# Value pass of a hybrid decoder block: the split weights of a pair of blocks, one block behind the other in place of side by side

## The chip, the cores and the metric

The kernel runs on one core of one Trainium2 chip. The core has a matrix engine (TensorE, PE in the profile; its weight loads have a row of their own, PEld), VectorE (DVE), ScalarE (ACT), GpSimd (POOL) and a queue engine (SyncE, SP) that issues transfers; 16 DMA engines move data between memory and the core's on-chip memory of 128 partitions. The metric is the device time of one launch in microseconds. Before the change it was 1544.01 us, the median of three runs (1541.96 to 1545.22).

## What is computed

One layer of a decoder block for 256 tokens of width 2048: sparse attention beside a convolution, a projection, a layer norm, then an expert channel mixer and a second layer norm. The change lies in the mixer. Each token picks, for each of 8 heads, 16 of 16384 experts; an expert has a row of `u_tab` and a row of `v_tab`.

```python
def peer_ffn(y, wq, sub_keys, u_tab, v_tab):
    ...
        top, pos = lax.top_k(cand, PK_TOPK)
        eidx = jnp.take_along_axis(cidx, pos, axis=-1)
        g = jax.nn.softmax(top.astype(jnp.float32), axis=-1)
        u = u_tab[eidx]
        v = v_tab[eidx]
        h = jax.nn.gelu(jnp.einsum('btd,bthkd->bthk', yb, u))
        return jnp.einsum('bthk,bthkd->btd', g * h, v).astype(y.dtype)
```

The second einsum is the value pass: for each token, the sum of its 128 chosen rows of `v_tab`, each with its weight `g * h`.

## The kernel before

The kernel goes through the mixer in three stages. The u pass reads all of `u_tab` in 128 blocks of 128 experts. The middle stage finds the weights and spreads them into a dense matrix. The value pass multiplies that matrix with all of `v_tab`.

The dense matrix is `W = wp.tile([P, T, P], F32)`: partition, 256 tokens `t`, 128 blocks `j`. On one partition the 128 blocks of a token lie side by side, so two tokens of the same block are 128 elements, 512 bytes, apart. Block `j` of the value pass takes the weights `W[:, t, j]` of all 256 tokens and the 128 rows of `v_tab` that belong to it. The first 768 columns of `v_tab` are not multiplied densely: they are gathered row by row and summed. The other 1280 (`VC`) go through TensorE, cut into pieces of 512, 512 and 256 columns (`blocks`).

TensorE works in a one-pass format (`F32R`), so each operand is split into a high part and the remainder. `mm3` (L330 to L332) multiplies high by high, high by low and low by high. In the profile's names, L330 is `wh` with `vh`, L331 `wh` with `vl`, L332 `wl` with `vh`. The weights are the stationary operand: each matmul first loads 128 columns, one for each of 128 tokens, and then streams 512 or 256 columns of V. A block has 2 token halves x 3 pieces x 3 products = 18 matmuls; the result tiles are `f` (512 wide) and `fboth` (256 wide).

One turn `j` of the loop, in the order in which the program gives work to the engines, which each engine keeps:

- `v_load(j + 2)`: SP issues the transfer of the rows of block `j + 2` into `vr` (L1768, 640 KB, three buffers); POOL issues two gathers into `gv` (L1776, one for each token half, 384 KB each, eight buffers).
- `v_split(j + 1)`: on even blocks `v_rows` comes first and makes the weights of two blocks at once, high part `wh` on ScalarE (L1805), remainder `wl` on VectorE (L1806). Then `v_cols` makes `vh` on ScalarE (L1816) and the remainder `vl`, 1024 columns on VectorE and 256 on POOL (both L1821).
- `v_gather(j)`: VectorE adds the two gathered tiles into `pg` (L1781).
- `v_use(j)`: the 18 matmuls.

`vh` and `vl` have one buffer in each of two pools, used in turn by `j % 2`; `wh` and `wl` likewise by pair, `p % 2`. So `vh` of block `j + 1` waits until TensorE has finished with block `j - 1`, and a `vr` buffer is free when `vh` and both parts of `vl` have been made from it. Nine blocks (`AHEAD`) have one gather fewer in the loop; it was done ahead.

Of the kernel before, what the change touches and what calls it, by code (L numbers as in the profile page):

```python
# [10 lines left out]
F32R = mybir.dt.float32r  # L11
# [9 lines left out]
P = 128  # L21
T = 256
# [96 lines left out]
def tile_hybrid_block(  # L119
# [6 lines left out]
    x = x[0]  # L126
# [202 lines left out]
    def mm3(acc, ah, al, bh, bl, start, stop):  # L329
        nc.tensor.matmul(acc, lhsT=ah, rhs=bh, start=start, stop=False)  # L330
        nc.tensor.matmul(acc, lhsT=ah, rhs=bl, start=False, stop=False)  # L331
        nc.tensor.matmul(acc, lhsT=al, rhs=bh, start=False, stop=stop)  # L332
# [591 lines left out]
    if True:  # L924
# [14 lines left out]
        for c in range(8):  # L939
# [6 lines left out]
            src = raws[i][:, r * 512:r * 512 + 512]  # L946
# [408 lines left out]
    if True:  # L1355
# [96 lines left out]
        for h in range(1, PH):  # L1452
            for half in range(2):
                p = 2 * h + half
# [67 lines left out]
    W = wp.tile([P, T, P], F32, name="W")  # L1522
# [274 lines left out]
    halves_ = {}  # L1797

    def v_rows(p, tt):
        if p not in halves_:  # L1800
            halves_[p] = [vps[p % 2].tile([P, T, 2], F32R, name=f"w{x}{p}", tag=f"w{x}") for x in "hl"]
        s = slice(0, T) if tt is None else slice(tt * P, tt * P + P)
        wh, wl = (t[:, s] for t in halves_[p])
        src = W[:, s, 2 * p:2 * p + 2]
        nc.scalar.activation(wh, src, AF.Copy)  # L1805
        nc.vector.tensor_tensor(wl, src, wh.bitcast(F32), op=OP.subtract)  # L1806

# [15 lines left out]
    def v_split(j):  # L1823
        if j % 2 == 0:
            v_rows(j // 2, None)
        v_cols(j, slice(0, VC))
# [77 lines left out]
    if True:  # L1904
# [77 lines left out]
        for m in range(NQ - QP, NQ, 2):  # L1982
# [16 lines left out]
            if m == NQ - 12:  # L1999
                v_raw(2)  # L2000
                v_rows(0, 0)
# [7 lines left out]
            if m == NQ - QP + 2:  # L2009
# [5 lines left out]
                vps = [psv.enter_context(tc.tile_pool(name="vp0", bufs=1, reuse_waits="tile", side="right"))]  # L2015
# [6 lines left out]
    if stop == "u":  # L2022
        dump("hv", hv)
        if "H" in dbg:
# [6 lines left out]
    acc = [[psv_.tile([P, 512], F32, name=f"f{tt}{b}", tag=f"f{tt}{b}") for b in range(nb - 1)]  # L2031
           for tt in range(2)]
# [9 lines left out]
    def v_part(j, tt, b, stop=False):  # L2042
        (wh, wl), vhl = halves_[j // 2], parts[j]
        (a, e), s = blocks[b], slice(tt * P, tt * P + P)
        mm3(acc[tt][b], wh[:, s, j % 2], wl[:, s, j % 2], vhl[0][:, a:e], vhl[1][:, a:e],
            j == 0 and not (tt and b == nb - 1), stop)

    def v_use(j, tts=range(2)):
        for b in range(nb):
            for tt in tts:  # L2050
                v_part(j, tt, b)
# [10 lines left out]
    z2 = []  # L2062
    if True:
        v_rows(0, 1)
        for j in range(P):
            if j == 1:
# [8 lines left out]
            elif len(z2) < 2:  # L2075
                tt = len(z2)
# [35 lines left out]
        for j in (P - 2, P - 1):  # L2112
            for b in range(nb):
                v_part(j, 0, b, j == P - 1 and b < nb - 1)
        residual(nb - 1)
        for j in (P - 2, P - 1):
            v_part(j, 1, nb - 1, j == P - 1)
# [144 lines left out]
```

## Time and profile before

| What | Value |
|---|---|
| median of three runs | 1544.01 us |
| the profiled execution | 1547.76 us |
| its span (first to last instruction) | 1545.9 us |
| PE, PEld, DVE, ACT, POOL busy, of the span | 97, 89, 88, 55, 67% |
| granted TensorE clock, mean | 0.996 |
| DMA, mean over the span | 308 GB/s |
| first matmul of the value pass | 1052.9 us |
| last matmul of the value pass on these weights | 1534 us |

The stages, in us of the span, with the time that each engine was busy in them:

| Stage | us | PE | DVE | ACT | POOL | DMA share | GB/s |
|---|---|---|---|---|---|---|---|
| up to the u pass | 0 to 480 | 471.28 | 378.85 | 257.00 | 198.43 | 0.56 | 200 |
| u pass | 480 to 900 | 415.57 | 387.55 | 275.90 | 316.03 | 0.99 | 384 |
| middle | 900 to 1052 | 148.97 | 134.67 | 115.87 | 115.99 | 0.72 | 232 |
| value pass | 1052 to 1534 | 470.41 | 443.66 | 202.91 | 400.50 | 0.98 | 376 |
| last norm and output | 1534 to 1546 | 0.86 | 8.35 | 1.47 | 6.69 | 0.48 | 175 |

Matmuls overlap in the records: the next one starts before the last one's recorded end. A stage in which PE is "busy" nearly all the time may therefore still have room; the distance from one start to the next tells more. A wait is put down to what came last. The DMA share is the mean busy share of the 16 DMA engines.

### The profile page before, as it was taken

Reading aid. Unit: us, or ns where it says so; the run is one execution under the profiler, and the core shown is the slowest. Engines: PE = TensorE matmul, PEld = TensorE weight load, DVE = VectorE, ACT = ScalarE, POOL = GpSimd, SP = SyncE. Lnnn points to the kernel's source line nnn. Section 1 sums busy time; section 2 is a strip of 40 time slices with the busy share of each in tenths; the row PEclk is TensorE's granted clock in tenths of the full one; section 3 lists DMA queues with packets and bytes.
Section 4 is the critical chain, followed back from the end, with each engine's and each line's share of the span. In section 5 each row is a group of like instructions: output and inputs, shape, how many; then the busy total and the mean of one; then the engine's idle time right before and its main releaser. Section 6 shows DMA issues by size and latency. Waiting matters only on the chain.

```text
span 1545.9 us, 29511 instructions
## 1 busy us (share of the span) xinstructions
PE 1507.1 (97%) x10932; PEld 1379.0 (89%) x10932; DVE 1353.1 (88%) x2381; ACT 853.1 (55%) x1207; POOL 1037.7 (67%) x897
## 2 busy tenths in 40 slices
PE   9999999999999999999999999999999999999996
PEld 9998999987999999999999888887878888888885
DVE  5999777857599998999998789988999999989898
ACT  5355776645434666666666657885444444444443
POOL 1886000053774777777877678767888888888883
PEclk9999999999999999999999999999999999999999
DMA  9664545255685999999999987757999999999997
GB/s 350 226 243 137 174 138 186 89 194 187 217 303 171 406 403 403 404 401 395 398 407 389 363 285 250 225 194 257 395 370 389 394 380 385 386 384 407 379 389 256
DMA packets 101492, 475.77 MB, mean 308 GB/s; under 512 B 17728, under 2 KB 20516, under 8 KB 92772
## 3 DMA queue, kind: packets, MB, share of 16 engines
q1 hardware_dynamic: 59300, 252.81, 44.1%
q0 software_dynamic: 41040, 218.60, 37.4%
q10 hardware_dynamic: 1008, 2.49, 0.4%
q8 instruction: 85, 1.39, 0.4%
q14 instruction: 59, 0.48, 0.1%
HBM read 468.99 MB, written 4.85 MB: 307 GB/s over the span
## 4 chain that ended last, share of the span: by engine, by line
PE 32%; DMA 12%; issue 9%; POOL 6%; DVE 6%; ACT 3%; DVEq 0%; SPq 0%; POOLq 0%; ACTq 0%
PE hp L1541 8%; PE hp L1537 8%; PE hp L1538 8%; DMA vr<-in_v_dense_dram 7%; POOL gv L1776 4%; PE bank L1703 4%; DVE pg L1781 3%; DMA gv<-in_v_rows_dram,e 3%; PE bank L1751 2%; POOL vl L1821 2%; DMA ur<-in_u_dense_dram 1%; DVE vl L1821 1%; ACT vh L1816 1%; PE bank L1733 1%; ACT slot L1739 1%
## 5 line engine op out<-in xcount | busy, mean ns | idle before, releaser
L1776 POOL DMA_INDIRECT gv<-in_v_rows_dram,e x256 | 292.2, 1141 | 67.5 <-issue 32.8
L1816 ACT ACTIVATE vh<-vr 128x1280 fp32r<-128x1280 f32 (+1 forms) x129 | 162.1, 1258 | 271.8 <-DMA vr<-in_v_dense_dram 199.7
L291 POOL TENSOR_TENSOR lo<-raw,hi 128x1024 fp32r<-128x1024 f32 (+1 forms) x76 | 171.8, 2273 | 166.0 <-ACT hi L273 165.4
L1537 PE MATMUL hp<-yh,uh 128*128 128x256 f32 x1152 | 280.6, 283 | 1.1 <-ACT uh L1240 1.1
L1538 PE MATMUL hp<-yl,uh 128*128 128x256 f32 x1152 | 280.1, 282 | 0.0
L1173 POOL DMA_INDIRECT gu<-in_u_rows_dram,e x196 | 192.8, 983 | 98.8 <-DVE gu L1183 62.3
L1781 DVE SCALAR_TENSOR_TENSOR pg<-gv,hv,pg 128x768 f32<-128x768 f32 x247 | 251.7, 1019 | 4.3
L1240 ACT ACTIVATE uh<-ur 128x1152 fp32r<-128x1152 f32 x128 | 149.6, 1168 | 130.6 <-PE hp L1538 45.6
L331 PE MATMUL f<-vl,wh 128*128 128x512 f32 x512 | 209.6, 409 | 10.8 <-DVE vl L1821 10.1
L1537 PEld LDWEIGHTS hp<-yh,uh 128*128 128x128 f32 x1152 | 217.8, 189 | 1.5 <-ACT uh L1240 1.5
L1538 PEld LDWEIGHTS hp<-yl,uh 128*128 128x128 f32 x1152 | 217.8, 189 | 0.0
L273 ACT ACTIVATE hi<-raw 128x1024 fp32r<-128x1024 f32 (+1 forms) x134 | 138.1, 1036 | 127.5 <-PE pwq L331 27.4
L1183 DVE SCALAR_TENSOR_TENSOR gu<-gu,yp 128x896 f32<-128x896 f32 x196 | 206.3, 1077 | 0.1
L330 PE MATMUL f<-vh,wh 128*128 128x512 f32 x512 | 204.4, 399 | 0.8 <-ACT vh L1816 0.8
L332 PE MATMUL f<-vh,wl 128*128 128x512 f32 x512 | 203.4, 397 | 0.0
L1821 DVE TENSOR_TENSOR vl<-vr,vh 128x1024 fp32r<-128x1024 f32 (+1 forms) x129 | 160.7, 1247 | 30.8 <-ACT vh L1816 30.0
L1541 PE MATMUL hp<-yh,ul 128*128 128x256 f32 x1152 | 157.8, 282 | 0.8 <-DVE ul L1245 0.8
L1245 DVE TENSOR_TENSOR ul<-ut,uh 128x768 fp32r<-128x768 f32 x126 | 119.6, 949 | 31.1 <-ACT ut L1244 22.9
L1541 PEld LDWEIGHTS hp<-yh,ul 128*128 128x128 f32 x1152 | 145.6, 188 | 1.2 <-DVE ul L1245 1.2
L1246 POOL TENSOR_TENSOR ul<-ur,uh 128x384 fp32r<-128x384 f32 x128 | 131.3, 1026 | 17.7 <-ACT uh L1240 15.1
L331 PEld LDWEIGHTS f<-vl,wh 128*128 128x128 f32 x512 | 100.1, 195 | 42.7 <-DVE vl L1821 27.3
L1821 POOL TENSOR_TENSOR vl<-vr,vh 128x256 fp32r<-128x256 f32 (+1 forms) x129 | 123.1, 954 | 12.8 <-ACT vh L1816 10.3
(390 smaller groups left out, 3857.9 us busy)
## 6 DMA issues: line engine op xcount, KB each, us to landing
vr<-in_v_dense_dram SPq DMA_DIRECT2D x128, 640.0 KB
ur<-in_u_dense_dram SPq DMA_DIRECT2D x128, 576.0 KB
raw<-in_w_pieces_dram SPq DMA_DIRECT2D x62, 1024.0 KB
gv<-in_v_rows_dram,e POOLq DMA_INDIRECT x256, 7.0
gu<-in_u_rows_dram,e POOLq DMA_INDIRECT x196, 6.8
raw<-in_w_pieces_dram SPq DMA_DIRECT2D x5, 512.0 KB
raw<-in_w_pieces_dram SPq DMA_DIRECT2D x4, 608.0 KB
w1k<-in_cmp_w_dram SPq DMA_DIRECT2D x1, 2048.0 KB
```

The source lines that it names most:

```text
L330: nc.tensor.matmul(acc, lhsT=ah, rhs=bh, start=start, stop=False)
L331: nc.tensor.matmul(acc, lhsT=ah, rhs=bl, start=False, stop=False)
L332: nc.tensor.matmul(acc, lhsT=al, rhs=bh, start=False, stop=stop)
L1173: nc.gpsimd.indirect_dma_start(out=gt, out_offset=None, in_=u_rows, in_offset=bass.IndirectOffsetOnAxis(ap=fl(e4, tt)[:, c:c + 1], axis=0))
L1183: nc.vector.scalar_tensor_tensor(gt, gt, 1.0, yr, op0=OP.mult, op1=OP.mult, accum_out=hv[:, tt, c:c + 1])
L1537: nc.tensor.matmul(acc, lhsT=uh[:, s], rhs=chunk(yh, k), start=k == 0, stop=False)
L1538: nc.tensor.matmul(acc, lhsT=uh[:, s], rhs=chunk(yl, k), start=False, stop=False)
L1541: nc.tensor.matmul(acc, lhsT=ul[:, s], rhs=chunk(yh, k), start=False, stop=k == UK - 1)
L1776: nc.gpsimd.indirect_dma_start(out=gvs[j, tt], out_offset=None, in_=v_rows_, in_offset=bass.IndirectOffsetOnAxis(ap=fl(e4, tt)[:, j:j + 1] ...
L1781: engine.scalar_tensor_tensor(pg[:, tt], gvs.pop((j, tt)), wv[:, tt, j:j + 1], pg[:, tt], op0=OP.mult, op1=OP.add)
L1816: nc.scalar.activation(vh, src[:, s], AF.Copy)
L1821: e.tensor_tensor(vl, src[:, c], vh.bitcast(F32), op=OP.subtract)
```

## The change

`wh` and `wl` of a pair of blocks were `[P, T, 2]`: for each token the weights of the two blocks side by side. They become `[P, 2, T]`: all 256 tokens of the first block, then all 256 of the second.

```diff
@@ def v_rows(p, tt):
-            halves_[p] = [vps[p % 2].tile([P, T, 2], F32R, name=f"w{x}{p}", tag=f"w{x}") for x in "hl"]
+            halves_[p] = [vps[p % 2].tile([P, 2, T], F32R, name=f"w{x}{p}", tag=f"w{x}") for x in "hl"]
         s = slice(0, T) if tt is None else slice(tt * P, tt * P + P)
-        wh, wl = (t[:, s] for t in halves_[p])
-        src = W[:, s, 2 * p:2 * p + 2]
+        wh, wl = (t[:, :, s] for t in halves_[p])
+        src = W[:, s, 2 * p:2 * p + 2].rearrange("p t j -> p j t")
         nc.scalar.activation(wh, src, AF.Copy)
         nc.vector.tensor_tensor(wl, src, wh.bitcast(F32), op=OP.subtract)
@@ def v_part(j, tt, b, stop=False):
-        mm3(acc[tt][b], wh[:, s, j % 2], wl[:, s, j % 2], vhl[0][:, a:e], vhl[1][:, a:e],
+        mm3(acc[tt][b], wh[:, j % 2, s], wl[:, j % 2, s], vhl[0][:, a:e], vhl[1][:, a:e],
             j == 0 and not (tt and b == nb - 1), stop)
```

So L1805 and L1806 read the same 512 elements of `W` in another order: before, for each token two neighbours; now, for one block all tokens and then for the other, each element 512 bytes behind the last. They write `wh` and `wl` from front to back in both versions. A weight load of TensorE read 128 elements 8 bytes apart; now it reads 128 neighbours. The tiles keep their size and buffers, and every engine has the same instructions in the same order. The first pair's weights are made in two steps of 128 tokens each (`v_rows(0, 0)`, `v_rows(0, 1)`); there the two blocks' parts are written 256 elements apart.

## The prediction

> **What bounds the kernel now.** The whole change lies in the value pass, so I read that stage by itself: its busy times in one window, the chain that ended last inside it (shares by line), and who waited for whom (us in total, times, longest).
>
> ```profile
> core 0: us, PE busy (x) PEld busy (x) DVE busy (x) ACT busy (x) POOL busy (x), PEclk, DMA share, GB/s
> 1060.00:1520.00 460.00, 449.05 (x2214) 377.39 (x2214) 426.17 (x430) 192.12 (x185) 394.33 (x364) 1.00 0.99 384
> ```
>
> ```profile
> by line: issue 27.4%; DMA vr<-in_v_dense_dram 24.4%; POOL gv L1776 12.4%; DVE pg L1781 8.9%; DMA gv<-in_v_rows_dram,e 8.6%; POOL vl L1821 6.9%; DVE vl L1821 3.4%; ACT vh L1816 2.7%; PE f L331 1.0%; PE f L332 0.9%; DMA z<-y_dram 0.9%; PE f L
> ```
>
> ```profile
> ACT vh L1816 <- DMA vr<-in_v_dense_dram: 199.7, 92, 3.8
> ACT vh L1816 <- PE fboth L332: 34.8, 16, 4.0
> PEld f L331 <- DVE vl L1821: 27.3, 58, 1.8
> PE f L331 <- DVE vl L1821: 10.1, 22, 1.5
> ```
>
> The first row is the steady part of the pass: DMA share 0.99, VectorE busy 426 of 460 us (93%), ScalarE only 192. PE shows 449, but matmuls overlap in the records, so its starts are counted below instead. The chain ("by line") hardly touches PE, some 1% for each of its lines; it runs through POOL's gather issues and the transfers of vr. The waits say the same: ScalarE waits 199.7 us for rows of V, 34.8 us for PE to release a buffer, and PE waits 27.3 + 10.1 us for VectorE's vl. One turn of the timeline (start in us, us taken, engine, line) shows how these hang together:
>
> ```profile
> 1302.14 0.66 ACT L1805 ACTIVATE wh<-W 128x512 fp32r<-128x512 f32 x1
> 1304.33 0.75 POOL L1821 TENSOR_TENSOR vl<-vr,vh 128x256 fp32r<-128x256 f32 x1
> 1305.11 0.33 SPq L1768 DMA_DIRECT2D vr<-in_v_dense_dram  x1
> 1305.24 0.96 POOL L1776 DMA_INDIRECT gv<-in_v_rows_dram,e  x1 [0.16 <-issue]
> 1305.40 0.68 DVE L1806 TENSOR_TENSOR wl<-W,wh 128x512 fp32r<-128x512 f32 x1
> 1306.23 1.22 DVE L1821 TENSOR_TENSOR vl<-vr,vh 128x1024 fp32r<-128x1024 f32 x1 [0.16 <-ACT vh L1816]
> 1306.50 1.77 POOL L1776 DMA_INDIRECT gv<-in_v_rows_dram,e  x1 [0.30 <-issue]
> 1308.29 0.76 POOL L1821 TENSOR_TENSOR vl<-vr,vh 128x256 fp32r<-128x256 f32 x1
> 1311.94 1.28 ACT L1816 ACTIVATE vh<-vr 128x1280 fp32r<-128x1280 f32 x1 [1.67 <-DMA vr<-in_v_dense_dram]
> ```
>
> The next vr is issued at 1305.11, just behind the end of POOL's vl (1304.33 + 0.75); the block it brings is converted at 1311.94, 6.83 us later. POOL's second gather took 1.77 us, not 0.96: it ran into VectorE's vl and ended 0.8 us behind it (1308.27 against 1307.45), and POOL's own vl came after. So **whatever delays VectorE's vl delays POOL, and through POOL the next transfer of V**.
>
> **What the change does, part by part.** No instruction is added, dropped or reordered on any engine. Three accesses change: ScalarE and VectorE write wh and wl contiguously, as before, but read W with one element every 512 bytes instead of two neighbours every 512 bytes; and TensorE loads its 128 weight columns 4 bytes apart instead of 8.
>
> **Read of W by VectorE.** Nothing in the trace is exactly this, so its neighbours, as groups (xcount, busy us, mean ns of one) and by tile (ns min/median/max):
>
> ```profile
> L1806 DVE TENSOR_TENSOR wl<-W,wh 128x512 fp32r<-128x512 f32 x63 | 43.8, 695 | 0.9 <-ACT wh L1805 0.9
> L1821 DVE TENSOR_TENSOR vl<-vr,vh 128x512 fp32r<-128x512 f32 x2 | 1.3, 672 | 0.0
> L482 DVE TENSOR_REDUCE csum<-conv 128x256 f32<-128x2048 f32 x1 | 3.9, 3851 | 0.5 <-ACT conv L469 0.5
> L763 DVE TENSOR_REDUCE st<-sc 128x4 f32<-128x1024 f32 x8 | 9.8, 1220 | 0.3
> L763 DVE TENSOR_REDUCE st<-sc 128x4 f32<-128x512 f32 x8 | 5.5, 686 | 0.3
> L570 DVE TENSOR_TENSOR blkk<-bk,small x8: 349/356/2534, 118.1 to 127.4; 128x120 f32<-128x120 f32 x8
> L710 DVE TENSOR_TENSOR csb<-csb,csm x4: 282/282/284, 198.0 to 284.5; 128x120 f32<-128x120 f32 x4
> ```
>
> Read in pairs, wl costs 695 ns, against 672 for the same subtraction on contiguous data: pairs are almost free. Single elements are not. L482 reads single elements 1 KB apart. The two L763 rows, contiguous, give (1220 - 686)/512 = 1.04 ns an element and 152 ns fixed, so its 2048 elements would take 2.29 us; it took 3.85, or 0.76 ns more for each. L570, a subtraction's sister with single reads 64 bytes apart, has a median of 356 ns where L710, of the same size, has 282: 0.62 ns more for each. On wl's 512 elements that is 0.39 or 0.32 us. I take **+0.35 us per wl**, between the two. The ends: 0, if a single read costs no more than a pair, and +0.53, if each element takes twice its 1.04 ns; it can hardly become faster, since wl stands 23 ns above the contiguous row.
>
> [...]
>
> **Read of W by ScalarE.** A wh starts at 1302.14 and ends at 1302.80; its wl starts at 1305.40. If it grew by 0.66 us, doubled, it would still end 1.9 us ahead. ScalarE is idle for 268 of the 460 us, over 2 us a block of some 3.7, so vh behind it is covered too: cost 0, and at most the doubling where a wh follows late.
>
> **What VectorE's 0.35 us does.** A pair of blocks on VectorE is one wl, two vl and four sums:
>
> ```profile
> 1254.24 0.68 DVE L1806 TENSOR_TENSOR wl<-W,wh 128x512 fp32r<-128x512 f32 x1
> 1254.84 1.22 DVE L1821 TENSOR_TENSOR vl<-vr,vh 128x1024 fp32r<-128x1024 f32 x1
> ...
> 1261.08 0.69 DVE L1806 TENSOR_TENSOR wl<-W,wh 128x512 fp32r<-128x512 f32 x1
> L1806 DVE TENSOR_TENSOR wl<-W,wh x63: 682/684/1142, 1057.8 to 1522.3; 128x512 fp32r<-128x512 f32 x63
> L1821 DVE TENSOR_TENSOR vl<-vr,vh 128x1024 fp32r<-128x1024 f32 x126 | 159.1, 1263 | 30.8 <-ACT vh L1816 30.0
> ```
>
> Without a gap a pair takes 1261.08 - 1254.24 = 6.84 us: VectorE's floor. The 63 wl stand (1522.3 - 1057.8)/62 = 7.49 us apart on average. The floor rises to 7.19, so VectorE alone is not the average bound, with 96% of the period taken instead of 91%. The cover is the idle time before vl, 30.8 us, or 0.5 us a pair. It isn't spread evenly: of the 62 periods between those wl starts, 27 are shorter than 7.19, and they fall short of it by 7.4 us in sum. These pairs are the ones that catch up behind a late transfer. If they are stretched to the new floor and nothing is made good later, the pass grows by 7.4 us; if the transfers (share 0.99) set the mean and a later issue only meets a shorter queue, by nothing; if every delay passes through, by 63 x 0.35 = 22 us. Since vr has three buffers and its next issue follows POOL's vl at once, I expect little to be made good: **+7 us**.
>
> **Weight loads of TensorE.**
>
> ```profile
> 324.74 0.40 PE L330 MATMUL mixb<-hi,ch 128*128 128x512 f32 x1
> 329.98 0.39 PE L332 MATMUL mixb<-hi,cl 128*128 128x512 f32 x1
> 1199.82 0.40 PE L331 MATMUL f<-vl,wh 128*128 128x512 f32 x1
> 1202.40 0.28 PE L330 MATMUL fboth<-vh,wh 128*128 128x256 f32 x1
> 1203.13 0.40 PE L330 MATMUL f<-vh,wh 128*128 128x512 f32 x1
> L330 PEld LDWEIGHTS mixb<-hi,ch x64: 186/188/192, 324.6 to 368.9; 128*128 128x128 f32 x64
> L330 PEld LDWEIGHTS f<-vh,wh x512: 192/195/329, 1052.9 to 1533.8; 128*128 128x128 f32 x171
> 700.66 0.28 PE L1537 MATMUL hp<-yh,uh 128*128 128x256 f32 x1
> 702.80 1.23 PE L1541 MATMUL hp<-yh,ul 128*128 128x256 f32 x9
> ```
>
> In the value pass a 512-wide matmul takes (1202.40 - 1199.82)/11 steps = 235 ns and a 256-wide one (1203.13 - 1202.40)/6 = 122. With contiguous weights the output projection's 512-wide ones take (329.98 - 324.74)/23 = 228, and the 256-wide ones of the u pass (702.80 - 700.66)/18 = 119; a weight load takes 188 ns there and 195 here. If the 8-byte step is the reason, a block's 12 wide and 6 narrow matmuls lose 12 x 7 + 6 x 3 = 0.10 us, 13 us over 128 blocks, and PE's floor for a pair falls from 2 x (12 x 0.235 + 6 x 0.122) = 7.10 us to 6.90. But PE has 3% of the chain, some 14 us, of which 7/235 is 0.4 us. Ends: 0, if something else makes 235 of 228, and -13, if PE set every block. I take **-0.5 us**.
>
> [...] The rows' 195 against 188 ns differ with the step, so I keep the row.
>
> At the start of the pass two 128x256 pieces of wh and wl are made on the way to the first matmul: 0.2 us at most, inside the rounding.
>
> **Sum.** +7 - 0.5 = +6.5 us. The profiled execution took 1547.8 us, so its like would take 1554.3; it lies 3.8 us above the median of the three runs, 1544.0. On that median the forecast is **1550 us**.
>
> **The rivals.**
>
> *The read costs nothing* (0.18). If single reads run at the pair's speed, or the layout reaches the engine in another order than written, VectorE is as before and PE gains off the path: 1543.5 us. For it: 695 against 672 ns shows VectorE swallowing 256 jumps. Against: L482 and L570.
>
> *PE's release sets the pace* (0.12), the other side. ScalarE waited 16 times for PE to free vh, 34.8 us. There PE's 0.10 us a block counts: 16 x 0.10 = 1.6 us, and the 8 periods near PE's floor (7.03 to 7.16) give up to 0.2 each, 1.6 more, with about 1 us where the block behind catches up sooner: 1540 us. It decides as long as wl stays below 0.695 + (7.10 - 6.84) = 0.95 us, where VectorE's new floor reaches PE's old one. L570's row puts wl at 1.01, L482's at 1.09, so it needs a penalty under two thirds of theirs.
>
> *Every delay passes through* (0.13). Each wl holds POOL's gather as vl does (1.77 against 0.96 us), POOL's vl and the next vr slip by the whole 0.35 us: +15 to +22, 1563 us with 19. For it: vr's issue follows POOL's vl within 0.03 us. Against: 30.8 us of idle before vl, in which delays vanish.
>
> **How the numbers follow.** My forecast has 0.57, with its own range of 1546 to 1556 (VectorE's price from 0.25 to 0.53 us, and half to all of it kept). With the rival without a cost and half of the faster one the range goes from 1541 to 1560; what is left out is the upper rival and the lower half of the faster one. A measurement of this kernel tells some 0.2%, 3 us, from no change. Faster: 0.12 and a quarter of the first rival, 0.17. Same: the rest of that rival and a tenth of the forecast, 0.20. Slower: 0.63.
>
> **What would show it.** Right: the group of wl at 1.0 to 1.1 us where it has 0.695; smallest distances of wl near 7.2 instead of 6.84; idle before vl well under 30.8 us; PE's waits for vl above 37 us in sum; weight loads at 188 ns and steps of 228. Wrong: wl still near 0.69 (the first rival); wl dearer but the pass no longer (the transfers absorb it); idle of PE down with a shorter pass (the second); POOL's gathers longer on average than now by 0.1 us or more (the third).

## The result, and the profile after

Six runs of the changed kernel have a median of 1561.32 us (1556.56 to 1568.58), six of the kernel before 1543.89 us (1538.89 to 1545.22). The ratio is 1.0102, with a 95% interval of 1.0075 to 1.0130: slower by 1%, some 16 us where 6.5 were forecast. On the median of the prediction's three runs that ratio gives 1559.8 us, the very top of its full range and above the forecast's own range of 1546 to 1556; the new median itself lies 1.3 us above both.

The profiled execution of the changed kernel is the slowest of its six (1568.58 us), and 8 us of that were there before the value pass began. So the lines below are of a second profile of the same kernel, the run `change_again`, which the last set of experiments held (1561.12 us, span 1559.3). There the value pass begins at 1053.4, where the kernel before begins at 1052.9, and from the first to the last start of its matmuls 494.3 us pass in place of 481.5: 12.8 of the 13.4 us between these two executions. First the busy times in the window that was shown of before (columns: PE, PEld, DVE, ACT, POOL, each with its count, clock, DMA share, GB/s):

```profile
1060.00:1520.00 460.00, 437.74 (x2159) 355.63 (x2158) 433.65 (x420) 215.05 (x182) 399.36 (x358) 1.00 0.98 374
```

In the same 460 us PE gets through 2159 matmuls in place of 2214, and the transfers through 374 GB/s in place of 384. VectorE's busy time rises from 426 to 434 us with fewer instructions, 420 for 430. The groups tell which (count, busy us, mean ns of one, idle before); the last line is `wh` in the kernel before:

```profile
L1821 DVE TENSOR_TENSOR vl<-vr,vh 128x1024 fp32r<-128x1024 f32 x126 | 156.2, 1240 | 23.5 <-ACT vh L1816 23.0
L1805 ACT ACTIVATE wh<-W 128x512 fp32r<-128x512 f32 x63 | 71.4, 1133 | 0.0
L1806 DVE TENSOR_TENSOR wl<-W,wh 128x512 fp32r<-128x512 f32 x63 | 68.5, 1088 | 1.4 <-ACT wh L1805 1.4
L1776 POOL DMA_INDIRECT gv<-in_v_rows_dram,e x250 | 309.1, 1236 | 59.5 <-issue 31.9 <-DVE pg L1781 12.9 <-DVE wl L1806 11.3
L1805 ACT ACTIVATE wh<-W 128x512 fp32r<-128x512 f32 x63 | 41.8, 663 | 0.0
```

`wl` takes 1088 ns where it took 695, `wh` 1133 where it took 663. VectorE's idle time ahead of `vl` went from 30.8 to 23.5 us. VectorE's timeline shows its new floor, a pair without a gap:

```profile
1290.90 1.08 DVE L1806 TENSOR_TENSOR wl<-W,wh 128x512 fp32r<-128x512 f32 x1
1291.90 1.21 DVE L1821 TENSOR_TENSOR vl<-vr,vh 128x1024 fp32r<-128x1024 f32 x1
1293.04 2.07 DVE L1781 SCALAR_TENSOR_TENSOR pg<-gv,hv,pg 128x768 f32<-128x768 f32 x2
1295.01 1.22 DVE L1821 TENSOR_TENSOR vl<-vr,vh 128x1024 fp32r<-128x1024 f32 x1
1296.15 2.08 DVE L1781 SCALAR_TENSOR_TENSOR pg<-gv,hv,pg 128x768 f32<-128x768 f32 x2
1298.13 1.07 DVE L1806 TENSOR_TENSOR wl<-W,wh 128x512 fp32r<-128x512 f32 x1
```

1298.13 - 1290.90 = 7.23 us, where 6.84 was the floor. 29 of the 62 distances between two `wl` now lie at it, between 7.20 and 7.26. The waits of the steady part (us in total, times, longest) show who is held up: PE, for `vl`, 67 us in place of 37.

```profile
PEld f L331 <- DVE vl L1821: 46.5, 79, 1.8
PE f L331 <- DVE vl L1821: 20.7, 43, 1.5
```

Last, the side that got cheaper, PE's timeline in the first profile of the changed kernel (start in us, us taken): the first of twelve wide matmuls in a row, and the narrow one that follows the twelfth.

```profile
1309.58 0.40 PE L330 MATMUL f<-vh,wh 128*128 128x512 f32 x1
1312.33 0.28 PE L330 MATMUL fboth<-vh,wh 128*128 128x256 f32 x1
```

A wide matmul takes (1312.33 - 1309.58)/12 = 229 ns, where it took 235. TensorE got faster; that the kernel gained nothing by it, loads_alone shows below.

### The profile page after: what moved, and what is told of

It reads as the page before. It is cut to its first block, busy times and chain, and to the rows that moved or that the text cites. A ratio compares the mean times of both kernels' runs of the same rounds, so it can differ in the third digit from the quotient of the medians.

```text
span 1566.8 us, 29511 instructions
## 1 busy us (share of the span) xinstructions
PE 1512.3 (97%) x10932; PEld 1370.3 (87%) x10932; DVE 1375.5 (88%) x2381; ACT 883.2 (56%) x1207; POOL 1049.6 (67%) x897
## 4 chain that ended last, share of the span: by engine, by line
PE 30%; DMA 12%; issue 9%; DVE 9%; POOL 5%; ACT 3%; DVEq 0%; SPq 0%; POOLq 0%; ACTq 0%
DMA vr<-in_v_dense_dram 8%; PE hp L1541 7%; PE hp L1537 7%; PE hp L1538 7%; PE bank L1703 4%; DVE pg L1781 4%; POOL gv L1776 2%; PE bank L1751 2%; DMA gv<-in_v_rows_dram,e 2%; DMA ur<-in_u_dense_dram 2%; DVE vl L1821 2%; DVE wl L1806 2%; ACT vh L1816 1%; POOL vl L1821 1%; PE bank L1733 1%
## 5 line engine op out<-in xcount | busy, mean ns | idle before, releaser
L1776 POOL DMA_INDIRECT gv<-in_v_rows_dram,e x256 | 311.2, 1216 | 67.7 <-issue 29.6
L1816 ACT ACTIVATE vh<-vr 128x1280 fp32r<-128x1280 f32 (+1 forms) x129 | 162.1, 1258 | 254.7 <-DMA vr<-in_v_dense_dram 171.0
L331 PEld LDWEIGHTS f<-vl,wh 128*128 128x128 f32 x512 | 96.1, 188 | 65.2 <-DVE vl L1821 48.5
L1821 POOL TENSOR_TENSOR vl<-vr,vh 128x256 fp32r<-128x256 f32 (+1 forms) x129 | 116.2, 900 | 13.3 <-ACT vh L1816 10.9
```

Source lines behind the costliest of these rows:

```text
L1776: nc.gpsimd.indirect_dma_start(out=gvs[j, tt], out_offset=None, in_=v_rows_, in_offset=bass.IndirectOffsetOnAxis(ap=fl(e4, tt)[:, j:j + 1] ...
L1816: nc.scalar.activation(vh, src[:, s], AF.Copy)
L1821: e.tensor_tensor(vl, src[:, c], vh.bitcast(F32), op=OP.subtract)
```

## The experiments

My theory: VectorE's dearer read of W is the whole loss, and the contiguous loads are off the path. The rivals: ScalarE's dearer `wh` makes a part of it; PE's release of `vh` sets the pace; what hurts is not VectorE's time but that a longer `wl` keeps POOL's gathers out for longer. Three sets of four kernels ran on three chips, whose medians for the kernel before are 1560, 1548 and 1546 us; only ratios are compared, each to the kernel before on its own chip. The last three columns come from one profiled execution of each kernel. The kernel before was profiled on one chip only, so small differences in these columns between chips say little.

| Run | Ratio, 95% interval | `wl`, ns | `vl` on VectorE, mean ns | mean distance of two `wl`, us |
|---|---|---|---|---|
| the kernel before | 1 | 695 | 1263 | 7.49 |
| loads_alone | 1.0008 (0.9987 to 1.0028) | 691 | 1234 | 7.42 |
| vector_read_alone | 1.0103 (1.0075 to 1.0131) | 1102 | 1239 | 7.64 |
| scalar_read_alone | 1.0029 (1.0011 to 1.0047) | 688 | 1258 | 7.46 |
| vector_time_alone | 1.0166 (1.0135 to 1.0197) | 685 | 1291 | 7.75 |
| pairs_read_split_write | 1.0080 (1.0060 to 1.0100) | 1125 | 1238 | 7.67 |
| copy_by_scalar | 1.0003 (0.9985 to 1.0021) | 696 | 1249 | 7.42 |
| no_wl | 0.9949 (0.9931 to 0.9967) | none | 1231 | (7.23, every second `vl`) |
| vector_time_behind | 1.0204 (1.0180 to 1.0227) | 773 | 1501 | 8.06 |
| change_again | 1.0107 (1.0084 to 1.0131) | 1088 | 1240 | 7.69 |
| vector_time_holding | 1.0331 (1.0288 to 1.0374) | 738 | 1639 | 8.30 |
| vector_time_small | 1.0043 (1.0026 to 1.0060) | 701 | 1265 | 7.61 |
| no_wl_loads | 0.9949 (0.9932 to 0.9967) | none | 1232 | (7.28, every second `vl`) |

In the code below a line of three dots marks what is left out, and the line that makes the tile `idle` is left out throughout. The run change_again is the changed kernel itself, with no edit, on the third chip:

> The changed kernel once more, beside the next three on one chip. Both theories: +0.8 to +1.2% against before, wl at 1.09 us, weight loads at 188 ns.

1.0107 beside 1.0102: the loss is the same on another chip.

### The three parts of the change, one by one

TensorE alone: the tiles are written as before, and TensorE reads them as if they lay block by block.

```diff
+    def blk(t, j):
+        return t.rearrange("p t j -> p (t j)")[:, j % 2 * T:j % 2 * T + T]
...
-        mm3(acc[tt][b], wh[:, s, j % 2], wl[:, s, j % 2], vhl[0][:, a:e], vhl[1][:, a:e],
+        mm3(acc[tt][b], blk(wh, j)[:, s], blk(wl, j)[:, s], vhl[0][:, a:e], vhl[1][:, a:e],
```

> The kernel before, in which TensorE alone reads its weight columns as 128 neighbours, out of tiles that are still written side by side; so the matmuls use the wrong weights for half of the columns, and the values of the dense part are not the reference's. wh and wl cost what they did (0.66 and 0.69 us). Theory (VectorE's dearer read is the whole loss, the loads are off the path): weight loads at 188 ns, wide matmuls 228 ns apart in place of 235, and the time within 0.2% of before, -3 to +1 us. Rival (PE's release of vh sets the pace): -0.4 to -0.8%, 6 to 13 us less.

1.0008: nothing, with an interval from -0.1 to +0.3%. The edit did its work: a weight load took 188 ns in the median, as after the change. The rival that PE sets the pace asked for 0.4 to 0.8% less, and falls. The waits for PE's release of `vh` are no measure of this: they are 34.8 us before and 8.9 here, but 46.2 and 22.3 in two profiles of the changed kernel.

VectorE alone, in the old layout:

```diff
         nc.scalar.activation(wh, src, AF.Copy)
+        wh, wl, src = (t.rearrange("p t j -> p j t") for t in (wh, wl, src))
         nc.vector.tensor_tensor(wl, src, wh.bitcast(F32), op=OP.subtract)
```

> The kernel before with the old layout, in which VectorE alone goes through its subtraction block by block: single elements of W 512 bytes apart, wh read and wl written 8 bytes apart. Theory: wl at 1.09 us as after the change, smallest distance of two wl 7.23 us, and all of the loss or a little more, since TensorE's gain is missing: +1.0 to +1.3%, 15 to 20 us. Rival (ScalarE's dearer wh, 1.13 us, makes a part of the loss): +0.5% or less.

```profile
L1807 DVE TENSOR_TENSOR wl<-W,wh 128x512 fp32r<-128x512 f32 x63 | 69.4, 1102 | 0.9 <-ACT wh L1805 0.9
```

1.0103, the change's own 1.0102 and 1.0107 (in this kernel `wl` stands at L1807). ScalarE is as before, so its part is not needed to make the loss.

ScalarE alone, in the old layout:

```diff
-        nc.scalar.activation(wh, src, AF.Copy)
+        nc.scalar.activation(wh.rearrange("p t j -> p j t"), src.rearrange("p t j -> p j t"), AF.Copy)
```

> The kernel before with the old layout, in which ScalarE alone goes through its conversion block by block: single elements of W 512 bytes apart, wh written 8 bytes apart. Theory: wh at about 1.13 us, hidden in ScalarE's idle time; the time within 0.2% of before. Rival (ScalarE's dearer wh delays vh and with it the turn): +0.3 to +0.6%, 5 to 9 us.

Neither quite: 1.0029, 2 to 7 us by the interval, more than my 0.2% at its middle and just under the rival's 0.3 to 0.6%. `wh` took 1149 ns. I return to it below.

### Is it VectorE's time, or POOL kept out?

An added instruction with the same time, which reads the accumulator memory:

```diff
         nc.vector.tensor_tensor(wl, src, wh.bitcast(F32), op=OP.subtract)
+        if tt is None:
+            nc.vector.bn_stats(idle, pg[:, 0, :300])
```

> The kernel before with one more instruction on VectorE behind each full wl: statistics over 300 columns of pg, which lie in the accumulator memory, into a tile that nothing reads; some 0.47 us, 0.38 from start to start, as much as the change adds to wl. It has no second operand in the memory that POOL reads. Theory (what counts is VectorE's time ahead of vl): the same loss as the change or more, +0.9 to +1.3%. Rival (what counts is that a longer wl blocks POOL's gathers longer): under half of it, +0.2 to +0.5%.

1.0166, more than the change, from an instruction that reads nothing in the memory that POOL reads. So a loss of this size needs no longer hold by `wl`; another instruction's time on VectorE, with what it brings, is enough. POOL isn't cleared by that, for its gathers took 1199 ns on average in this run too, where they take 1147 before; they were longer with either kind of delay on VectorE (1236 in change_again). And the loss was larger than I expected, so how the time is added counts too: 19 of its `vl` took more than 1.3 us, where the kernel before has 9. Two runs went after that: the same statistics behind `vl`,

```diff
+        if j % 2 == 0:
+            nc.vector.bn_stats(idle, pg[:, 0, :300])
```

> As vector_time_alone, with the same statistics over 300 columns of pg, but behind vl of the even blocks in place of ahead of it: the same VectorE time a pair, and vl not pushed back directly. Theory (VectorE's time counts through its floor, wherever it stands): +1.0 to +1.7%, like vector_time_alone. Rival (it counts only where it stands between the sums and vl, since vl leads to POOL and the next transfer): +0.2 to +0.6%.

and behind `wl` again, in place of the statistics, an addition of two pieces of W:

```diff
+        if tt is None:
+            flat = W.rearrange("p t j -> p (t j)")
+            nc.vector.tensor_tensor(idle, flat[:, :312], flat[:, 512:824], op=OP.add)
```

> As vector_time_alone (behind each full wl), but the added instruction adds two contiguous pieces of W, 312 columns each, 0.47 us: the same VectorE time, with two operands in the memory that POOL reads, as wl has. The sum is read by nobody. Theory (an instruction of that kind keeps POOL's off VectorE's vl, as a longer wl does): vl at 1.24 us on average and the loss of vector_read_alone, +0.8 to +1.2%. Rival (only VectorE's time counts): vl at 1.29 us and +1.4 to +1.9%, as vector_time_alone.

Both missed, upwards: 1.0204 and 1.0331. I had thought that an instruction of the second kind would shield `vl` as a longer `wl` does. The mean of `vl` says the opposite: 1501 and 1639 ns, where 1220 is usual. One stretch of vector_time_holding shows what happens (VectorE and POOL in order of time; L1824 is `vl`'s line in this kernel):

```profile
1406.81 0.69 DVE L1806 TENSOR_TENSOR wl<-W,wh 128x512 fp32r<-128x512 f32 x1
1406.92 1.39 POOL L1776 DMA_INDIRECT gv<-in_v_rows_dram,e  x1 [0.30 <-DVE pg L1781]
1407.41 0.48 DVE L1809 TENSOR_TENSOR idle<-W 128x312 f32<-128x312 f32 x1
1407.81 2.37 DVE L1824 TENSOR_TENSOR vl<-vr,vh 128x1024 fp32r<-128x1024 f32 x1
1408.33 0.74 POOL L1824 TENSOR_TENSOR vl<-vr,vh 128x256 fp32r<-128x256 f32 x1
```

The reader is to see that `vl` starts at 1407.81 and ends at 1410.18, 1.11 us behind the end of POOL's `vl` (1409.07). The gather on POOL began during `wl` and was still running, and POOL's `vl` followed it; by these times VectorE's `vl`, 1.22 us elsewhere, did nearly all of its work after both were done. My reading, which no run shows by itself, is that a seam between two VectorE instructions lets POOL in, and that what comes next on VectorE pays. A POOL instruction that is running when `vl` starts is not a mark of it by itself: nearly all of the 80 `vl` above 1.3 us in this run had one, and all 9 of the kernel before, but so had 112 and 102 of all 126. For the reading speaks that a `wl` that merely takes longer adds no seam, and `change_again` has only 6 such `vl`. That the number of seams explains the whole difference between 1.0166 and 1.0331 was not tried by itself.

These two runs also went round another loop than the change. ScalarE waited for PE to release `vh` for 201 and 182 us in all, where it was 34.8 before and 22.3 and 46.2 in the two profiles of the changed kernel (below, first vector_time_behind, then vector_time_holding):

```profile
ACT vh L1816 <- PE fboth L332: 201.0, 81, 4.5
ACT vh L1819 <- PE fboth L332: 182.1, 69, 4.0
```

PE's waits for `vl` are 97 and 122 us there. By these waits a late `vl` held up PE, and PE held up the next `vh`. So they do not price the change; they price another instruction. Behind `vl` the statistics also took 0.50 us from start to start, where behind `wl` they took 0.39.

### How the loss grows

Half the added time (the edit beside vector_time_alone):

```diff
-            nc.vector.bn_stats(idle, pg[:, 0, :300])
+            nc.vector.bn_stats(idle, pg[:, 0, :108])
```

> As vector_time_alone with statistics over 108 columns in place of 300: 0.27 us, some 0.18 from start to start, half of the change's addition; VectorE's floor 7.02 us. Theory (the loss grows faster than the added time, since idle time ahead of vl swallows small additions): under +0.6%. Rival (each added microsecond costs its full share): +0.7 to +0.9%, half of vector_time_alone.

VectorE relieved, `wl` made for the first two pairs only:

```diff
...
-        nc.vector.tensor_tensor(wl, src, wh.bitcast(F32), op=OP.subtract)
+        if p < 2:
+            nc.vector.tensor_tensor(wl, src, wh.bitcast(F32), op=OP.subtract)
```

> The kernel before without the remainders of the weights from the third pair of blocks on: VectorE makes wl for two pairs only, and TensorE goes on using those two, so the product with wl is wrong. VectorE has 0.6 us a pair less, floor 6.24 us. Theory (the pass grows and shrinks with VectorE's time, half of which passes through): -0.4 to -1.0%, 6 to 16 us. Rival (transfers and TensorE already set the pass, and VectorE matters only above its present load): -0.3 to 0%.

The same, with the weights read block by block as in loads_alone:

> As no_wl (remainders of the weights for two pairs only), and TensorE reads its weight columns as 128 neighbours, as in loads_alone; the dense part uses wrong weights. VectorE's floor is 6.24 us and TensorE's 6.9 in place of 7.1. Theory (with VectorE relieved, TensorE's loads reach the path): -0.8 to -1.4% against before, at least 0.3% below no_wl. Rival (the transfers hold the pass there): as no_wl, -0.3 to -0.7%.

1.0043 for a floor of 7.01 us: 6.7 us for 63 x 0.17 = 10.7 us added, 62%, with 38 to 87% by the interval. The change adds 63 x 0.39 = 25 us and loses 16, 64%, about the same share. So +0.43% is under the 0.6% that I expected, but it does not show that the loss grows faster than the time. Taking 0.6 us a pair away, 37 us, gave only 7.9 us, 21%; with that edit POOL's gathers were shorter too, 976 ns on average where they take 1147. So VectorE already set a part of the pass before the change; below its old load other things take over soon, and above it most of what was added was paid. With VectorE relieved TensorE's loads are worth nothing that could be measured either (0.9949 twice): my expectation there missed. The rival, that the transfers hold the pass, stands, with a DMA share of 0.99 and 1.00 between 1060 and 1520 us in these two kernels; it was not tested by itself.

### Can the layout be had without the price?

The old order of reading into the new layout, so that writes jump instead of reads (this edit and the next are of the changed kernel):

```diff
-        src = W[:, s, 2 * p:2 * p + 2].rearrange("p t j -> p j t")
+        src = W[:, s, 2 * p:2 * p + 2]
+        wh, wl = (t.rearrange("p j t -> p t j") for t in (wh, wl))
```

> The change's layout, filled in the old order of reading: W in neighbouring pairs, wh and wl written (and wh read by VectorE) one element in each half by turns, 1 KB apart. TensorE has its contiguous weights. Theory (each step to another place of the memory costs VectorE time unless two elements lie together): wh as an operand jumps at every element, so wl stays near 1.09 us and the time at +0.8 to +1.2%. Rival (only the far-strided read of W is dear): wl at 0.70 us, and the time that of loads_alone, within 0.3% of before.

1.0080, with `wl` at 1125 ns and ScalarE's `wh` at 1146, although both read W in pairs. On ScalarE jumping at every element cost as much where it is written as where it is read; for VectorE, which here also reads `wh` in jumps, the two were not taken apart.

ScalarE makes a contiguous copy first, and both parts are made from it:

```diff
+        if tt is None:
+            wc = vps[p % 2].tile([P, 2, T], F32, name=f"wc{p}", tag="wc")
+            nc.scalar.activation(wc, src, AF.Copy)
+            src = wc
         nc.scalar.activation(wh, src, AF.Copy)
```

> The change's layout, with one more step on ScalarE: it first copies the pair's 512 elements of W, block by block, into a contiguous tile; wh and wl are then made from that tile. ScalarE's copy takes 1.13 us and its wh 0.61, both in its idle time; VectorE's wl reads and writes contiguously, 0.67 us; TensorE's weights are contiguous. Theory: VectorE's floor is back at 6.82 us and the loss is gone, -0.3 to +0.2% against before. Rival (ScalarE's longer work is a part of the loss, as scalar_read_alone hints with +0.3%): +0.3 to +0.7%.

```profile
L1807 ACT ACTIVATE wc<-W 128x512 f32<-128x512 f32 x63 | 71.8, 1139 | 0.0
L1810 DVE TENSOR_TENSOR wl<-wc,wh 128x512 fp32r<-128x512 f32 x63 | 43.9, 696 | 2.0 <-ACT wh L1809 2.0
L1809 ACT ACTIVATE wh<-wc 128x512 fp32r<-128x512 f32 x63 | 39.8, 633 | 2.0
```

1.0003. These are groups of that run: ScalarE works 1139 + 633 ns a pair where it worked 663, `wl` is back at 696, and the loss is gone while the weights are contiguous. That undoes the change's price, and it is no gain. It also speaks against ScalarE: with 1.1 us more a pair there is no loss here, so the 0.3% of scalar_read_alone does not come from ScalarE's time as such. What it does come from stays open; its mean distance of two `wl`, 7.46 us, does not show it either. No version that beats the kernel before came out of this; no_wl is faster but leaves work out.

## Why the prediction was right or wrong, point by point

**What bounds the pass: right as to VectorE and PE.** VectorE's `vl` was on the way to the end, and PE was not: vector_read_alone makes the whole loss, PE's waits for `vl` rose from 37 to 67 us with the change, and PE's faster loads moved nothing in loads_alone and no_wl_loads. That a delay of `vl` goes on through POOL to the next transfer of V was not shown by itself.

**The price of the read: right in kind, somewhat too low.** I took 0.35 us between two rows; 1088 - 695 = 0.39 was measured, which is what the reduction over single elements (L482) gave, not the short subtraction (L570). Single elements were dearer than pairs on ScalarE as well: `wh` went from 663 to 1133 ns.

**ScalarE's part: covered, as said, but not shown whole.** `wh` grew by 0.47 us, where the doubling that I had named as the end was 0.66. copy_by_scalar hid more than that, while scalar_read_alone lost 0.3% with 0.49 us more, for a cause that stays open.

**What VectorE's time does: this term of the sum was mis-sized, +7 us where 12 to 16 were measured.** I let the pairs below the new floor rise to it and left the longer ones as they were, +7. On the two profiles: the sum over the 62 distances of what lies under 7.23 us fell from 8.4 to 0.4 us, so that lifting gave 8 us. But the distances above 7.23 did not stay: their excess grew from 24.7 to 28.7 us. Together 12 us, and 12.8 between first and last matmul. So the longer distances grew too; that they did because the delay had also gone into POOL's `vl` and the next issue is argued, not shown. The loss of 16 us lies inside the +15 to +22 of the rival that passes every delay on, and 1561.3 is nearer to its 1563 than to my 1550. Not every delay passed, though: 25 us were added to `wl` and 64% of them paid. My own range ended at 1556; the full range's 1560 was not worked out from a row, and that it caught 1559.8 is luck.

**Weight loads: right in the rows, and 0 in the time.** The step of 8 bytes is the reason for 235 against 228 ns: with the step gone the loads take 189 ns on average where they took 196, as their row in the first profile of the changed kernel shows, and the wide matmuls 229; loads_alone, where nothing else changed, has the same 189, and its recorded wide `wh` with `vh` matmuls a median of 392 ns, as in the changed kernel, where the kernel before has 398.

```profile
L330 PEld LDWEIGHTS f<-vh,wh 128*128 128x128 f32 x512 | 96.6, 189 | 19.4 <-ACT vh L1816 2.4 <-issue 0.2
```

**The signs that I named** came as said: `wl` in 1.0 to 1.1, smallest distances near 7.2 (but for one of 6.98), idle before `vl` down, waits of PE up, wide matmuls 229 ns apart. The third rival's sign, gathers longer by 0.1 us, came just short: POOL's gathers took 1236 ns on average in change_again and 1223 in the first profile of the changed kernel, where the row of before has 1147.

```profile
L1776 POOL DMA_INDIRECT gv<-in_v_rows_dram,e x248 | 284.5, 1147 | 58.7 <-issue 31.3 <-DVE pg L1781 18.0 <-DMA vr<-in_v_dense_dram 4.0
```

How much of the loss comes by way of POOL and how much by way of PE's waits was not taken apart.

## What to carry to other kernels

Before a layout is changed for the reader that looks most important, count what the writer's access becomes: here 7 ns off each of the 36 loads of a pair of blocks, on an engine with room, was paid with 0.39 us a pair on an engine with little. Read the floor of every engine from start to start in a stretch without gaps, and compare it with the mean turn; here an engine at 91% of it paid for most of what was added, before it was at 100%. Where such a step must be made, try it on the engine with idle time: in copy_by_scalar 1.1 us more a pair on ScalarE cost nothing that could be measured, and 0.39 us on VectorE cost 1%. It has to be measured all the same, for scalar_read_alone lost 0.3%.

## What the runs showed of the hardware that was not expected

Instructions of VectorE and of POOL took longer beside each other, in both directions, and the time shows up as a longer instruction, not as a wait: in vector_time_holding a `vl`, 1.22 us elsewhere, took 2.37 beside a gather and a subtraction of POOL, and in the kernel before a gather took 1.77 us beside a `vl`, where another took 0.96. An instruction of 0.39 to 0.50 us from start to start, put between two others on VectorE, cost at least its own time in three kernels; the one of 0.17 us, in vector_time_small, cost 62% of it. The statistics took 0.39 us from start to start behind `wl` and 0.50 behind `vl` (medians), 25 and 32 us for 63 of them, and the kernel lost 26 and 32. The addition of two pieces of W took 0.40, 25 us, and the kernel lost 51.

On ScalarE writing in jumps was as dear as reading in jumps: its 512 elements took 1133 ns read singly and written in order, 1146 read in pairs and written in jumps, and 663 read in pairs and written in order. The two prices did not add up: read singly and written 8 bytes apart (scalar_read_alone) they took 1149.
